# A two-layer decoder trunk on one core: the evictions and the split weights beside the RWKV-7 recurrence, kept in the order of emission

## The chip, the cores and the metric

The kernel runs on 1 core of a Trainium2 chip. The metric is device time in microseconds (us) of one execution; lower is better. TensorE is PE in the profile, VectorE is DVE, ScalarE is ACT, GpSimd is POOL and SyncE, whose queue issues most of the transfers, is SP.

## The reference, cut to what matters

The trunk has two layers of width 1024 over 1024 positions, batch 1, in float32. Layer 0 mixes tokens with a gated MLP, layer 1 with RWKV-7 time mixing; each layer then has a squared-ReLU MLP (1024 to 4096 to 1024). The change is about layer 1's mixer:

```python
def rwkv7_mixer(h, mu, w_in, w0, w1, w2, a0, a1, a2, g1, g2, k_k, k_a, r_k, ln_g, ln_b, w_out):
    xx = token_shift(h) - h
    xr, xw, xk, xv, xa, xg = [h + xx * mu[i] for i in range(6)]
    r, k, v = xr @ w_in[:, 0], xk @ w_in[:, 1], xv @ w_in[:, 2]
    w_log = -jax.nn.softplus(-(w0 + jnp.tanh(xw @ w1) @ w2)) - 0.5
    a = jax.nn.sigmoid(a0 + (xa @ a1) @ a2)
    g = jax.nn.sigmoid(xg @ g1) @ g2
    ...
    # for each head of 64, state S (64 x 64), over all positions:
    #   S = S * w_t + (S a_t) b_t^T + v_t k_t^T ;  y_t = S r_t
    y = wkv7_scan(rh, decay, kh, vh, -kk, kk * ah)
    ...
    return (y * g) @ w_out
```

## The kernel before

**Numbers in two parts.** PE multiplies float32 values in a rounded form. So that the large products keep their precision, each weight tile and each activation tile is split into a rounded part (`hi`) and the rest (`lo`), and three matmuls (hi by hi, hi by lo, lo by hi) stand for one. A *piece* is a 128x512 weight tile. To split one on chip, `split_piece` casts it (`wh`, on ACT or every third time on DVE, L401) and subtracts (`wl`, on DVE or POOL in turn, L407).

**Layer 1's mixer works on four quarters q of 256 positions.** `jobs` (L810) lists the products of a quarter: `big` (r, k, v, four jobs `m` each), `hidden` (the first factor of w, a or g) and `outs` (the second factor). Each gathers its inputs from `mixes` (token-shifted blends, DVE and POOL, split by `split_pair` into `xi`), multiplies into a PSUM bank named `acc` (two buffers), and `out2` evicts the bank into an `ev` tile (three buffers, L931 and L989) and stores it in DRAM. `outp` multiplies the recurrence's gated output, which `gated` loads from DRAM (`ev<-yd`, L995), with the last weight.

**The weights of the mixer are used once in each quarter.** `presplit` therefore splits all 80 pieces of quarter 0 ahead, beside the end of layer 0, and stores both parts in DRAM (`split`, from the tiles `ada_acc` and `araw`, L336, L355, L358). From quarter 1 on `load_split` (L326) brings both parts back: two transfers of 256 KB for one piece, and no work of another engine.

**The recurrence runs beside these products.** `wkv` cuts it into 16 units (a quarter q and four heads, m). A unit is a set of generators: `unit_a` prepares the factors, `unit_s` inverts 16x16 triangular blocks on DVE (15 steps `pr`, `tb`, between a round trip through DRAM: `ltd<-la`, `lb<-ltd`, then `tpd<-tb`, `t<-tpd`, `pf<-tpd`), `unit_b` joins the blocks, `unit_c` runs four chunks of 64 positions in three steps each, and `unit_d` normalises and stores. In `unit_c` a step is: matmuls into the bank `c`, its eviction (`xs`, then `uv`, then the new state `S`), and the next step's matmuls read that.

**What sets the order.** `interleave` (L1211) holds a heap of the generators by due time, counted in units; each `yield` names the next due time, and a step is 1/13 of a unit (`SLOT`). Time goes forward by the nominal cost of the product work that it emits in between, `RATES` us of it to a unit (28.0 for the first ten units, 41.5 after). PE's instructions keep this order of emission (`Pinned`). Those of all other engines are ordered by a scheduler, which may move them past each other where no data forbid it. After the products come the second MLP's first blocks for the first half of positions (`half0`), then the rest of that MLP alone.

Of the kernel before, what the change touches and what calls it, by code (L numbers as in the profile page):

```python
# [16 lines left out]
P = 128  # L17
# [91 lines left out]
class Trunk:  # L109
# [219 lines left out]
    def presplit(self, todo, pool):  # L329
# [9 lines left out]
        todo = list(zip(todo, self.split_ahead))  # L339
# [28 lines left out]
    def make_split(self, dp):  # L368
# [9 lines left out]
        self.split_ahead = kept  # L378
        at = lambda kind, q: [j for j in self.jobs() if j[:2] == (kind, q)]
# [6 lines left out]
        self.order_split = [p for kind, _, name, m in self.parts()[1] for p in kept[place[kind, name, m]]]  # L386
# [423 lines left out]
    def jobs(self):  # L810


        for q in range(self.NQ):
            for name, low in ("vw", "ra", "kg"):
                for m in range(4):
                    yield "big", q, name, m
                    if m in (1, 2):
                        yield ("hidden", "outs")[m - 1], q, low, 0
        for q in range(2):
            for m in range(4):  # L820
                yield "outp", q, "", m
# [7 lines left out]
    def pieces(self, jobs):  # L829
# [3 lines left out]
        for kind, q, name, m in jobs:  # L833
# [12 lines left out]
            else:  # L846
                for h in range(2):
                    cs = slice(h * 512, h * 512 + 512)
                    if name == "g":
                        yield [a["b_g2"][:P, cs]], 0, None  # L850
                        yield [a["b_g2"][P:, cs]] * 3, 0, slice(64, 96)
                    else:
                        yield [a[f"b_{name}2"][:, cs]] * 2, 0, None
# [108 lines left out]
    def outs(self, q, name, _):  # L962
        nc = self.nc
        bias = {"w": self.w0h, "a": self.a0h, "g": None}[name]
        for m in range(4):
            if m % 2 == 0:
                wh, wl = self.piece()
                if name == "g":
                    gst, _ = self.piece()
# [215 lines left out]
    RATES = [28.0] * 10 + [41.5]  # L1185
# [25 lines left out]
    def interleave(self, gens, bg):  # L1211
# [4 lines left out]
        now = 0.  # L1216
        while live:
            due, n, t, g = live[0]
            if now < due:
                c = next(bg, None)  # L1220
                now = float("inf") if c is None else now + max(c, .01) / self.RATES[min(int(now), len(self.RATES) - 1)]
                continue
            try:
                heapq.heapreplace(live, [t + next(g), n, t, g])
            except StopIteration:
                heapq.heappop(live)

# [54 lines left out]
    def unit_a(self, d):  # L1282
# [39 lines left out]
        yield 0.2  # L1322
# [7 lines left out]
        yield 0.21  # L1330
        S.activation(rn, rn, AF.Exp, scale=-0.5)
        yield 0.25
# [3 lines left out]
        yield 0.28  # L1336
# [35 lines left out]
    def unit_e(self, d, z):  # L1372
# [10 lines left out]
        for c in range(4):  # L1383
            cc = (z * 4 + c) * 2
            PE.transpose(pt[:, c * P:(c + 1) * P], bk[:, cc:cc + 2].rearrange("p a t -> p (a t)"), self.ident)
        S.copy(tm[:, qc], pt.rearrange("p (c t) -> p c t", t=P))
# [17 lines left out]
    def unit_s(self, d):  # L1404
# [10 lines left out]
        yield 0.68  # L1415
        for i in range(1, NB):
# [6 lines left out]
            yield 0.68 + .017 * i  # L1423
        V.tensor_copy(tb[:, 1], tb[:, 0].rearrange("p s k -> p k s"))
        yield 0.96
# [3 lines left out]
        yield 1.0  # L1429
# [14 lines left out]
    def unit_b(self, d):  # L1444
# [15 lines left out]
        yield at(3) + .005  # L1460
# [3 lines left out]
        pw = self.ps("t")  # L1464
        pr, pq = cut(pw, 16), cut(pw[:, P:], 16)
# [5 lines left out]
        yield at(4) + .005  # L1471
# [12 lines left out]
        yield at(5) + .005  # L1484
# [10 lines left out]
        yield at(6) + .005  # L1495
        for s in self.HS:
            a, b = s.start, s.start + 32
            (S.copy if b > 64 else V.tensor_copy)(pf[a:b, :, 32:], pr[a:b])

    def unit_c(self, d):  # L1500
# [11 lines left out]
        for c in range(4):  # L1512
# [40 lines left out]
            yield step(3 * c + 3) if c < 3 else step(11) + .01  # L1553
# [240 lines left out]
```

## Time and profile before

| | |
|---|---|
| time, median of 3 runs | 2800.86 us (2793.97 to 2807.12) |
| the profiled execution's own time | 2805.26 us |
| its span, from the first to the last instruction | 2803.5 us |
| mean granted TensorE clock | 0.969 |
| PE busy | 2613.3 us, 93% |
| DVE, ACT, POOL busy | 1638.3, 1146.9, 544.7 us |
| moved by DMA | 483.67 MB, mean 173 GB/s |

The profile is of one execution. PE is busy when any matmul is in flight. The granted clock is the share of full speed at which TensorE was let run: it has two levels, 0.5 (1.2 GHz) and 1.0 (2.4 GHz), and a mean over a stretch tells how much of it was at the lower one. An engine's instructions run in its queue's order, so one that waits holds up all that stand behind it. The program's stages by time: layer 0's first mixer to 476 us, its MLP from there to about 1040 us with the splitting ahead beside it until 755 us, the mixer's quarter 0 until 1226 us, the recurrence with quarters 1 to 3 until about 1715 us, with `outp` and `half0` until 2340 us, and the rest of the second MLP to the end.

### The profile page before, as it was taken

What the parts mean: (1) busy time and instruction counts of PE and PEld (TensorE: products, weight loads), DVE (VectorE), ACT (ScalarE), POOL (GpSimd) and SP (SyncE); (2) the same over time, 40 slices, a digit from 0 to 9 for tenths busy, and PEclk for the clock granted to TensorE, in tenths of its full rate; (3) what the DMA queues carried; (4) which work ended last, traced back from release to release, by engine and by line L of the source; (5) the groups of instructions that cost most, each with busy time, mean ns of one, the idle gap of its engine ahead of it and who ended that gap; (6) DMA issues with size and microseconds to landing.
All of it is one profiled execution on the core that took longest, in us unless ns stands there. A gap on an engine that the chain in (4) does not pass through costs nothing.

```text
span 2803.5 us, 49454 instructions
## 1 busy us (share of the span) xinstructions
PE 2613.3 (93%) x19020; PEld 2152.6 (77%) x19020; DVE 1638.3 (58%) x3066; ACT 1146.9 (41%) x2074; POOL 544.7 (19%) x574
## 2 busy tenths in 40 slices
PE   6999999999999999787898997879999999999998
PEld 4788888877888788787787886777777778788887
DVE  7856775444333458866666663566667545744445
ACT  4523442333311344553454543464444334533333
POOL 1000000433300013431322231123334220100001
PEclk9999999999999999998999999899999999999999
DMA  7644545888711354788888889753333324333332
GB/s 279 211 142 128 167 155 163 274 278 255 237 49 49 91 165 138 241 291 261 260 284 265 270 289 274 211 149 110 104 104 100 91 86 151 103 109 94 95 94 83
DMA packets 369708, 483.67 MB, mean 173 GB/s; under 512 B 144320, under 2 KB 153536, under 8 KB 368704
## 3 DMA queue, kind: packets, MB, share of 16 engines
q1 hardware_dynamic: 354496, 454.18, 52.3%
q10 hardware_dynamic: 14976, 26.34, 2.5%
q8 instruction: 149, 2.44, 0.4%
q14 instruction: 87, 0.71, 0.1%
HBM read 390.07 MB, written 90.32 MB: 171 GB/s over the span
## 4 chain that ended last, share of the span: by engine, by line
PE 67%; DVE 12%; DMA 11%; ACT 4%; issue 4%; SPq 1%; POOL 1%; ACTq 0%; DVEq 0%; POOLq 0%
PE acc L448 24%; PE acc L646 15%; PE acc L103 15%; PE c L103 2%; PE acc L503 2%; DMA split<-ada_acc 2%; PE t L103 2%; DMA split<-araw 2%; DVE pr L1420 2%; DVE hm L874 2%; PE acc L894 1%; DVE wl L407 1%; DMA araw<-in_ada_w 1%; DVE xi L440 1%; DMA lb<-ltd 1%
## 5 line engine op out<-in xcount | busy, mean ns | idle before, releaser
L448 PE MATMUL acc<-h,wh 128*128 128x512 f32 x2112 | 667.4, 397 | 0.0
L401 ACT CAST wh<-raw 128x512 fp32r<-128x512 f32 x517 | 318.6, 619 | 732.6 <-PE acc L448 299.0
L646 PE MATMUL acc<-s,wh 128*128 128x512 f32 (+1 forms) x1664 | 510.4, 389 | 12.1 <-DVE s L439 9.1
L407 DVE TENSOR_TENSOR wl<-raw,wh 128x512 fp32r<-128x512 f32 x475 | 363.1, 767 | 264.4 <-ACT wh L401 259.3
L448 PEld LDWEIGHTS acc<-h,wh 128*128 128x128 f32 x2112 | 394.9, 188 | 94.5 <-issue 1.2
L448 PE MATMUL acc<-h,wl 128*128 128x512 f32 x1056 | 418.0, 396 | 0.0
L646 PEld LDWEIGHTS acc<-s,wh 128*128 128x128 f32 x1664 | 308.9, 189 | 86.5 <-DVE s L439 14.8
L646 PE MATMUL acc<-s,wl 128*128 128x512 f32 (+1 forms) x832 | 323.1, 389 | 0.5 <-DVE wl L407 0.5
L452 DVE SCALAR_TENSOR_TENSOR x<-acc,mod,x 128x512 f32<-128x512 f32 (+1 forms) x224 | 163.1, 730 | 231.0 <-PE acc L646 206.4
L448 PEld LDWEIGHTS acc<-h,wl 128*128 128x128 f32 x1056 | 198.4, 188 | 48.0 <-issue 0.5
L103 PE MATMUL acc<-s,wh 128*128 128x512 f32 (+1 forms) x616 | 188.0, 390 | 35.0 <-ACT s L437 18.3
L407 POOL TENSOR_TENSOR wl<-raw,wh 128x512 fp32r<-128x512 f32 (+1 forms) x107 | 145.6, 1363 | 318.2 <-ACT wh L401 156.2
L103 PE MATMUL acc<-xi,wh 128*128 128x256 f32 (+1 forms) x896 | 179.5, 300 | 10.0 <-ACT hm L954 5.2
L646 PEld LDWEIGHTS acc<-s,wl 128*128 128x128 f32 x832 | 157.5, 189 | 35.3 <-DVE wl L407 1.2
L358 POOL TENSOR_TENSOR araw<-araw,ada_acc 128x512 fp32r<-128x512 f32 (+1 forms) x78 | 101.2, 1300 | 389.4 <-ACT ada_acc L355 354.1
L103 PEld LDWEIGHTS acc<-s,wh 128*128 128x128 f32 x616 | 111.0, 196 | 62.8 <-ACT s L437 18.8
L103 PEld LDWEIGHTS acc<-xi,wh 128*128 128x128 f32 (+1 forms) x896 | 144.3, 198 | 17.7 <-ACT hm L954 5.4
L103 PE MATMUL acc<-h,wh 128*128 128x512 f32 (+1 forms) x512 | 150.7, 381 | 3.2 <-ACT ev L1057 3.2
L103 PE MATMUL acc<-xi,wl 128*128 128x256 f32 (+1 forms) x448 | 129.8, 290 | 1.6 <-issue 0.8
L355 ACT CAST ada_acc<-araw 128x512 fp32r<-128x512 f32 (+1 forms) x80 | 49.4, 618 | 168.4 <-DMA split<-ada_acc 124.3
L103 PE MATMUL acc<-s,wl 128*128 128x512 f32 (+1 forms) x308 | 114.9, 373 | 0.0
L157 DVE SCALAR_TENSOR_TENSOR ada_acc<-araw,cond,ada_acc 128x512 f32<-128x512 f32 x140 | 104.4, 746 | 13.0 <-DMA araw<-in_ada_w 11.1
(269 smaller groups left out, 4415.8 us busy)
## 6 DMA issues: line engine op xcount, KB each, us to landing
raw<-in_mlp_w SPq DMA_DIRECT2D x432, 256.0 KB, 2.7
araw<-in_ada_w SPq DMA_DIRECT2D x192, 256.0 KB, 3.5
raw<-split SPq DMA_DIRECT2D x142, 256.0 KB, 4.9
wh<-split SPq DMA_DIRECT2D x141, 256.0 KB, 4.6
wl<-split SPq DMA_DIRECT2D x141, 256.0 KB, 4.7
split<-ada_acc SPq DMA_DIRECT2D x76, 256.0 KB, 3.8
split<-araw SPq DMA_DIRECT2D x76, 256.0 KB, 4.1
araw<-in_w_in SPq DMA_DIRECT2D x48, 256.0 KB, 3.8
```

Source lines behind the costliest of these rows:

```text
L103: self.tc.keep_in_program_order(self.pe.matmul(*a, **k))
L157: nc.vector.scalar_tensor_tensor(acc, raw, self.cond[:, k:k + 1], acc, ALU.mult, ALU.add)
L355: nc.scalar.copy(hi[:rows, :m].bitcast(F32R), raw[:rows, :m])
L358: nc.gpsimd.tensor_tensor(to[lo, :m].bitcast(F32R), raw[lo, :m], hi[lo, :m], ALU.subtract)
L401: (nc.vector.tensor_copy if self.nhi % 3 == 0 and self.shared else nc.scalar.copy)(wh[:rows], raw[:rows])
L407: eng.tensor_tensor(wl[:rows], raw[:rows], rd(wh[:rows]), ALU.subtract)
L448: nc.tensor.matmul(ps, w[s](k), x[m][:, k], start=n == 0, stop=n == 3 * KC - 1)
L452: self.nc.vector.scalar_tensor_tensor(x[:, e], ps, gate[:, e:e + 1], x[:, e], ALU.mult, ALU.add)
L503: self.nc.tensor.matmul(ps, h[s][:, k, ts], self.wv[k][m], start=k + i == 0, stop=k + i == KC + 1)
L646: nc.tensor.matmul(ps, w[:, k], s[hf, k][:, i, ts], start=n == 0, stop=n == 3 * FB - 1)
L874: nc.vector.scalar_tensor_tensor(t[:, z], self.hx[:, e + z], self.mu[:, i, e + z:e + z + 1], self.h[:, e + z, 1:], ALU.mult, ALU.add)
L1420: V.tensor_tensor(pr[:, :i, :i], lb[:, 0:i, i].unsqueeze(1).to_broadcast([64, i, i]), tb[:, 0, 0:i, 0:i].rearrange("p s k -> p k s"), ALU. ...
```

## The change

It has five parts, all for the stretch in which the recurrence runs.

1. `pin` in `interleave`: each DVE, ACT and POOL instruction emitted there must follow, on its engine, the one emitted before it. The scheduler no longer reorders these three engines there. SP's transfers are not pinned.
2. Evictions are emitted later: extra `yield`s (+.012 of a unit, that is one more piece of product work) between a bank's matmuls and its eviction in `unit_c`, `unit_b`, `unit_e`; the triangular inverse starts at .745 of a unit and not .68, and hands over at 1.06 and not 1.0; some due times of `unit_a` move by .01 to .02.
3. One engine for each bank: the copies `uv`, `w1` and `pf`, of which DVE did one half of the partitions and ACT the other, are all ACT's; `pr` and `pq` get a bank each.
4. Fewer pieces are split ahead: of the pieces without repeats (`rep` 1) every second one (33 of the 80: 24 of `big`, 1 of `hidden`, 8 of `outp`) is left out of `presplit`, loaded raw each time, and split on chip by `split_piece`.
5. `outs` is cut into two jobs of two evictions each, after m = 2 and after m = 3 (before: one job of four evictions after m = 2). `RATES` becomes 27.3 and 42.5.

```diff
-        todo = list(zip(todo, self.split_ahead))
+        todo = [p for n, p in enumerate(zip(todo, self.split_ahead)) if n not in self.again]
...
+        self.again = {n for n, p in enumerate(self.whole) if p[1] == 1 and n % 2}
...
-        self.order_split = [p for kind, _, name, m in self.parts()[1] for p in kept[place[kind, name, m]]]
+        self.order_split = [self.whole[n] if n in self.again else kept[n]
+                            for kind, _, name, m in self.parts()[1]
+                            for n in range(place[kind, name, m].start, place[kind, name, m].stop)]
...
-                    if m in (1, 2):
-                        yield ("hidden", "outs")[m - 1], q, low, 0
+                    if m:
+                        yield "outs" if m > 1 else "hidden", q, low, max(m - 2, 0)
...
-    RATES = [28.0] * 10 + [41.5]
+    RATES = [27.3] * 10 + [42.5]
...
+        def pin():
+
+            nonlocal seen
+            assert nc.cur_bb is bb
+            ins = bb.bb.instructions
+            for i in ins[seen:]:
+                if i.engine in (E.DVE, E.Activation, E.Pool):
+                    if i.engine in last:
+                        self.tc.add_manual_dep(i, last[i.engine], mybir.DependencyInfo(
+                            mybir.DependencyClass.NoSync, mybir.DependencyReason.DATA), reason="order")
+                    last[i.engine] = i.name
+            seen = len(ins)
...
-        yield 0.68
+        yield 0.745
...
-        yield 1.0
+        yield 1.06
...
-        pw = self.ps("t")
-        pr, pq = cut(pw, 16), cut(pw[:, P:], 16)
+        pr, pq = cut(self.ps("t"), 16), cut(self.ps("r"), 16)
...
-            (S.copy if b > 64 else V.tensor_copy)(w[b:b + 32], pw[b:b + 32])
+            S.copy(w[b:b + 32], pw[b:b + 32])
...
+            yield step(3 * c) + .012
             xs = self.ups[1].tile([P, 2, CS], F32, name="xs", bufs=2)
...
+            yield step(3 * c + 1) + .012
             for z in Z:
-                (S.copy if z else V.tensor_copy)(uv[ss[z], z * 4 + c], pu[ss[z]])
+                S.copy(uv[ss[z], z * 4 + c], pu[ss[z]])
...
+            yield step(3 * c + 2) + .012
             for z in Z:
                 V.scalar_tensor_tensor(ns[z], pq[:, z * CS:z * CS + CS], gc[z], sg[z], ALU.mult, ALU.add)
```

The first place is ACT's queue in the second half of a unit (`xs`, `uv`: the recurrence's evictions; `xi`: a product's input; in brackets what each waits for, after the engine's or queue's name). Before:

```order
L437 CAST xi<-hm 128x512 [waits PE_49] x2
L1526 COPY xs<-c 128x128 [waits PE_49]
L931 COPY ev<-acc 128x512 [waits DMAHW2_49,PE_49]
L922 DMA sdk_8599<-ev 128x512 [waits DMAHW5_49,Activation_49]
L437 CAST xi<-hm 128x512 [waits DVE_49] x2
L1540 COPY uv_13518<-c 64x128 [waits DVE_49]
```

With the change:

```order
L1550 COPY xs<-c 128x128 [waits PE_49]
L441 CAST xi<-hm 128x512 [waits DVE_49]
L405 CAST wh<-raw 128x512 [waits DMAHW2_49,DMAHW0_49,PE_49]
L441 CAST xi<-hm 128x512 [waits DVE_49]
L1565 COPY uv_12440<-c 64x128 [waits PE_49]
L1565 COPY uv_12440<-c 64x128
```

Both halves of `uv` stand together and wait for PE instead of DVE; a weight's cast has come between, and the casts of `xi`, two at a time before, stand one by one.

The second place is POOL's queue over about half a unit (`sg`: the decayed state of a chunk; `k`, `bk`, `ar`, `ysq`: the recurrence's factors and its output). Before:

```order
L1584 TENSOR_TENSOR ysq<-ysq,gt 128x512
L1530 TENSOR_SCALAR sg<-S,g_11806 128x64 x2
L1315 TENSOR_SCALAR k_13568<-wa,kah,ka_8534 128x256 x2
L1316 TENSOR_TENSOR k_13568<-k_13568,k 128x512
L1329 TENSOR_TENSOR bk<-k_13568,gi 128x2x128
L1329 TENSOR_TENSOR bk<-k_13568,gi 128x2x2x64
L1530 TENSOR_SCALAR sg<-S,g_11806 128x64 x4
```

With the change:

```order
L1610 TENSOR_TENSOR ysq<-ysq,gt 128x512
L411 TENSOR_TENSOR wl<-raw,wh 128x512
L1554 TENSOR_SCALAR sg<-S,g_12436 128x64 x2
L411 TENSOR_TENSOR wl<-raw,wh 128x512
L1318 MEMSET g_14157 128x8
L1554 TENSOR_SCALAR sg<-S,g_12436 128x64 x2
L1338 TENSOR_SCALAR k_14234<-wa,kah,ka_8303 128x256 x2
L1339 TENSOR_TENSOR k_14234<-k_14234,k 128x512
L411 TENSOR_TENSOR wl<-raw,wh 128x512
L1352 TENSOR_TENSOR bk<-k_14234,gi 128x2x128
L1352 TENSOR_TENSOR bk<-k_14234,gi 128x2x2x64
```

Three subtractions for weights have come between the recurrence's own steps.

The third place is SP's queue where `outp` begins (`hm<-xd`: four loads of the first half of x, 512 KB each, into the space that the mixes leave; `ev<-yd`: the gated output that the first product of `outp` reads). Before:

```order
L1428 DMA tpd_257<-tb 64x16x16 x2
L326 DMA wl<-split_1_232 128x512
L1133 DMA hm<-xd 128x1024
L1433 DMA t<-tpd_257 64x8x64 x2
L1433 DMA pf_17741<-tpd_257 64x8x64 x2
L1133 DMA hm<-xd 128x1024 x3
L995 DMA ev<-yd_8607 128x512 x3
```

With the change:

```order
L1135 DMA hm<-xd 128x1024
L326 DMA raw<-split_1_223 128x512
L1591 DMA gt<-sdg_8363 128x512
L326 DMA wh<-split_0_224 96x512
L305 DMA raw<-in_b_w_out 128x512
L1452 DMA tpd_257<-tb 64x16x16 x2
L326 DMA wh<-split_0_225 128x512
L326 DMA wl<-split_1_226 128x512
L1457 DMA t<-tpd_257 64x8x64 x2
L1457 DMA pf_17634<-tpd_257 64x8x64 x2
L326 DMA raw<-split_0_229 128x512
```

The last of the four loads of x stands here ahead of the round trip of `tpd` (the other three stand 18 to 26 places further ahead); `ev<-yd` follows two transfers behind these rows.

## Rows read from the trace of the kernel before

**Rows 1.** The page: the span, and PE's busy time.

```profile
span 2803.5 us, 49454 instructions
PE 2613.3 (93%) x19020; PEld 2152.6 (77%) x19020; DVE 1638.3 (58%) x3066; ACT 1146.9 (41%) x2074; POOL 544.7 (19%) x574
```

**Rows 2.** Windows by stage: stretch, busy us of PE, PEld, DVE, ACT, POOL, clock, DMA.

```profile
476.00:720.00 244.00, 234.18 (x993) 187.14 (x993) 107.02 (x128) 84.71 (x147) 89.52 (x69) 0.99 0.82 263
1040.00:1226.00 186.00, 160.06 (x984) 141.92 (x982) 146.45 (x219) 87.12 (x155) 79.81 (x80) 0.92 0.63 193
1226.00:1715.00 489.00, 431.19 (x5767) 388.99 (x5766) 298.07 (x735) 240.07 (x476) 127.47 (x152) 0.94 0.87 278
1715.00:1950.00 235.00, 183.37 (x2157) 158.02 (x2156) 128.15 (x309) 107.53 (x217) 58.34 (x70) 0.88 0.60 177
1950.00:2340.00 390.00, 382.82 (x3700) 292.64 (x3699) 237.78 (x523) 160.51 (x305) 131.81 (x139) 1.00 0.37 105
```

**Rows 3.** Waits of PE, 1226 to 1715 us: us in total, times, longest.

```profile
PE acc L103 <- ACT ev L989: 10.8, 8, 3.0
PE t L103 <- DMA t<-tpd: 9.8, 2, 9.4
PE c L103 <- DVE S L1551: 9.0, 7, 2.7
PE c L103 <- ACT uv L1540: 5.9, 3, 3.0
PE acc L103 <- ACT ev L931: 5.3, 5, 2.8
```

**Rows 4.** Waits of PE, 1715 to 1950 us.

```profile
PE acc L103 <- ACT s L437: 20.2, 3, 17.2
PE acc L103 <- DVE hm L452: 10.4, 9, 2.9
```

**Rows 5.** Waits of ACT and of DVE, 1226 to 1715 us.

```profile
ACT uv L1540 <- DVE uv L1540: 55.1, 27, 6.5
...
DVE tb L1418 <- DMA lb<-ltd: 24.5, 5, 6.2
DVE xi L440 <- ACT xi L437: 22.4, 12, 8.5
```

**Rows 6.** Groups by line, 1226 to 1715 us: busy us, mean ns, idle before.

```profile
L1540 DVE COPY uv<-c 64x128 f32<-64x128 f32 x28 | 8.0, 285 | 29.7 <-PE c L103 29.5
L1540 ACT COPY uv<-c 64x128 f32<-64x128 f32 x28 | 7.3, 259 | 55.1 <-DVE uv L1540 55.1
```

**Rows 7.** Timeline of SP at the start of `outp`: start, us.

```profile
1740.95 2.63 SPq L1133 DMA_DIRECT2D hm<-xd  x3
1743.68 1.52 SPq L995 DMA_DIRECT2D ev<-yd  x3
```

**Rows 8.** Timeline of PE at the same place, and at 686 us.

```profile
1751.08 1.31 PE L103 MATMUL acc<-s,wh 128*128 128x256 f32 x2 [17.18 <-ACT s L437]
...
686.20 0.49 PE L646 MATMUL acc<-s,wh 128*128 128x512 f32 x1 [3.92 <-DVE s L439]
```

**Rows 9.** The casts of the splitting ahead, by source line.

```profile
L355 ACT CAST ada_acc<-araw x80: 513/620/627, 488.9 to 755.0; 128x512 fp32r<-128x512 f32 x76, 128x384 fp32r<-128x384 f32 x2, 96x512 fp32r<-96x512 f32 x2
```

**Rows 10.** Groups, 1090 to 1226 us: every piece is split on chip there.

```profile
L894 PE MATMUL acc<-xi,wl 128*128 128x256 f32 (+1 forms) x184 | 57.0, 310 | 17.9 <-DVE wl L407 10.1 <-POOL wl L407 7.7
L407 POOL TENSOR_TENSOR wl<-raw,wh 128x512 fp32r<-128x512 f32 (+1 forms) x29 | 39.6, 1371 | 64.9 <-ACT wh L401 41.9 <-DVE wh L401 18.5 <-PE acc L980 2.8
L401 ACT CAST wh<-raw 128x512 fp32r<-128x512 f32 (+2 forms) x39 | 23.6, 613 | 23.3 <-DMA raw<-in_w_in 8.1 <-PE acc L894 5.0 <-DMA raw<-in_mlp_w 3.8
```

**Rows 11.** Timeline of ACT: the first and last of one pair of table loads.

```profile
1755.78 1.28 ACT L1324 ACT_TABLE_LOAD   x1
...
1759.08 0.63 ACT L1331 ACTIVATE rn<-rn 128x512 f32<-128x512 f32 x1
```

**Rows 12.** One DVE instruction of each unit, 1226 to 1715 us: first and last start.

```profile
L1309 DVE TENSOR_TENSOR_SCAN wa<-rmask,wa x9: 1204/1220/1225, 1248.4 to 1714.8; 128x512 f32<-128x512 f32 x9
```

**Rows 13.** Transfers of weights, 1226 to 1715 us: KB each, us to landing.

```profile
raw<-split SPq DMA_DIRECT2D x113, 256.0 KB, 4.9
wh<-split SPq DMA_DIRECT2D x113, 256.0 KB, 4.7
```

More of the change, by code (lines that the diff above doesn't have):

```diff
@@ L846, in pieces @@
             else:
[L847 to L853, printed above, removed]
+                cs = slice(m * 512, m * 512 + 512)
+                if name == "g":
+                    yield [a["b_g2"][:P, cs]], 0, None
+                    yield [a["b_g2"][P:, cs]] * 3, 0, slice(64, 96)
+                else:
+                    yield [a[f"b_{name}2"][:, cs]] * 2, 0, None
     def load_h(self, q):
@@ L960, in hidden, with outs @@
                 nc.vector.tensor_tensor(gh[32:64, 2], s[32:64], rd(gh[32:64, 2]), ALU.subtract)
-    def outs(self, q, name, _):
+    def outs(self, q, name, part):
         nc = self.nc
         bias = {"w": self.w0h, "a": self.a0h, "g": None}[name]
[L965 to L969, printed above, removed]
+        wh, wl = self.piece()
+        if name == "g":
+            gst, _ = self.piece()
+        for m in range(2 * part, 2 * part + 2):
             ps, half = self.acc2()
@@ L1216, in interleave @@
         now = 0.
+        nc = self.nc
+        E = mybir.EngineType
+        last, bb = {}, nc.cur_bb
+        seen = len(bb.bb.instructions)
+        def pin():
[9 more added lines that the diff above has]
+            seen = len(ins)
         while live:
@@ L1221, in interleave @@
                 now = float("inf") if c is None else now + max(c, .01) / self.RATES[min(int(now), len(self.RATES) - 1)]
+                pin()
                 continue
@@ L1226, in interleave @@
                 heapq.heappop(live)
+            pin()
+        pin()
     def after(self, ins):
@@ L1321, in unit_a @@
         S.activation(g[:, :, 1:], c8(ew), AF.Exp, scale=-E)
-        yield 0.2
+        yield 0.18
         with self.after(self.last_ln):
@@ L1329, in unit_a @@
             G.tensor_tensor(bv[:, js, at], c2(k2)[:, js], c2(gi)[:, js], ALU.mult)
-        yield 0.21
+        yield 0.19
         S.activation(rn, rn, AF.Exp, scale=-0.5)
-        yield 0.25
+        yield 0.27
         V.scalar_tensor_tensor(kk, rn, 1e12 * 2.0 ** 8, kk, ALU.min, ALU.mult)
@@ L1335, in unit_a @@
         V.scalar_tensor_tensor(b2, kk, 2.0 ** -9, gi, ALU.mult, ALU.mult)
-        yield 0.28
+        yield 0.295
         for js, at in ((slice(0, 2), outer), (slice(2, 4), inner)):
@@ L1385, in unit_e @@
             PE.transpose(pt[:, c * P:(c + 1) * P], bk[:, cc:cc + 2].rearrange("p a t -> p (a t)"), self.ident)
+        yield t0 + .015
         S.copy(tm[:, qc], pt.rearrange("p (c t) -> p c t", t=P))
@@ L1422, in unit_s @@
             V.tensor_reduce(tb[:, 0, i, 0:i], pr[:, :i, :i], AX.X, ALU.add)
-            yield 0.68 + .017 * i
+            yield 0.745 + .017 * i
         V.tensor_copy(tb[:, 1], tb[:, 0].rearrange("p s k -> p k s"))
-        yield 0.96
+        yield 1.02
         td = self.tpd[d["n"] % 2]
@@ L1459, in unit_b @@
                           start=True, stop=True)
-        yield at(3) + .005
+        yield at(3) + .015
         w = self.ups[0].tile([P, 8, 16], F32, name="w0")
@@ L1470, in unit_b @@
                 PE.matmul(pq[a:a + 32, c], pf[a:a + 32, c, :32], w[a:a + 32, c], start=True, stop=True)
-        yield at(4) + .005
+        yield at(4) + .015
         for a, b in blocks[::2]:
@@ L1483, in unit_b @@
                 PE.matmul(pw[b:b + 32, c], lt(slice(a, b), c)[:, 32:], t[a:b, c, :32], start=True, stop=True)
-        yield at(5) + .005
+        yield at(5) + .015
         w = self.ups[0].tile([P, 8, 32], F32, name="w1")
@@ L1494, in unit_b @@
                 PE.matmul(pr[a:b, c], w[b:b + 32, c], pf[b:b + 32, c, 32:], start=True, stop=True)
-        yield at(6) + .005
+        yield at(6) + .015
         for s in self.HS:
             a, b = s.start, s.start + 32
-            (S.copy if b > 64 else V.tensor_copy)(pf[a:b, :, 32:], pr[a:b])
+            S.copy(pf[a:b, :, 32:], pr[a:b])
     def unit_c(self, d):
@@ L1552, in unit_c @@
             st = ns
-            yield step(3 * c + 3) if c < 3 else step(11) + .01
+            yield step(3 * c + 3) if c < 3 else step(11) + .025
         y = d["y"] = self.late("y")
```

## The prediction

> **What bounds the kernel now.** I read the page first: PE is busy for 2613.3 of 2803.5 us [rows 1], so no more than about 190 us of waiting can be won, and the count of matmuls does not change. Then the windows by stage, which tell where that waiting is [rows 2]. Look at PE's busy time and at the clock. Up to 1040 us there is little (476 to 720 us: 244.0 - 234.2 = 9.8 us idle). From 1226 to 1715 us, the recurrence beside quarters 1 to 3, PE idles 489.0 - 431.2 = 57.8 us, and the granted clock is 0.94: of 431 busy us some 6% is work done at 1.2 GHz that full speed would have saved, 26 us. From 1715 to 1950 us it is 51.6 us idle at 0.88, so 22 us more. From 1950 to 2340 us PE idles 7.2 us at full clock: PE itself is the bound. The clock falls behind idle time in these rows, so I charge each idle us there with 83.8 / 57.8 = 1.45 us. No other engine is the bound: between 1226 and 1715 us DVE is busy 61%, ACT 49%, POOL 26%. DMA, at 0.87, is the fullest, but PE hardly waits for weights.
>
> Then PE's waits in these two stretches. In the first they are many and short [rows 3]: evictions of `outs` (10.8 us), one late `t` (9.4 of 9.8 us), the recurrence's `S` and `uv` (14.9 us together), evictions of `big` (5.3 us); these are 40.8 of 57.8 us. In the second, one wait of 17.2 us stands out, where `outp` begins, and nine short ones on the residual [rows 4].
>
> **The change, part by part**, with minus for time saved.
>
> *Fewer pieces split ahead.* 80 casts take from 488.9 to 755.0 us, 3.33 us a piece [rows 9]; 47 pieces end near 645 us. The 33 casts, 33 subtractions, 66 stores and 33 loads that go lie beside PE's work and cost nothing, since ACT is busy only 35% there [rows 2]. What they do cost is the stall at 686 us, 3.92 us [rows 8], where a cast that waits for its store holds up ACT. It falls behind the new end: 3.92 x 1.45 = **-6**. Ends: 0 (the stall comes back elsewhere) and -14 (all 9.8 us).
>
> *One engine for a bank.* The two halves of `uv` take 0.285 us on DVE and then 0.259 us on ACT, in series: ACT stood still 55.1 us, 27 times, for DVE's half, 2.0 us each [rows 5, 6]. On ACT alone a pair is 0.52 us, with no handing over. PE's waits on `uv` and `S` are 14.9 us [rows 3]; I take half, 7.5 x 1.45 = **-11**; ends 0 and -22. ACT gets one more copy of 0.26 us for each pair, 7 us in the stretch, hidden by its 51% of idle time; if that cover went, the copy would be on the recurrence's chain. The Trainium skill (PSUM — Partial Sum Buffer, "PSUM bank collisions raise a hardware error") speaks against this part: two engines may be in one bank at once if they are in different quadrants of 32 partitions, and the halves are, so a pair on two engines would need only the longer copy. The trace does not show that use: ACT's half waits for DVE's. By that rule the pair would go from 0.285 to 0.52 us, 6.5 us over 28 pairs, and this term would be about zero.
>
> *`outs` in halves.* Four evictions in a row meet three `ev` tiles and two banks; two and two do not. I take two thirds of the 10.8 us: 7 x 1.45 = **-10**; ends 0 and -16.
>
> *The order.* The trace of before cannot show it. In the best case all other short waits go (57.8 - 10.8 - 9.8 - 14.9 = 22.3 us, -32). In the other direction the engines are coupled: each `xi` subtraction on DVE now stands right behind its cast on ACT, as the first place of the order shows. DVE waits so 12 times now, 22.4 us, 1.9 us each [rows 5]; 64 such casts fall into the stretch, and 64 x 1.9 = 120 us of waiting would fit into DVE's 191 us of idle time, but if a tenth reaches PE it costs +17. I take **-14**, nearer to the first end, since three engines then serve PE's needs in PE's own order. Later evictions belong here: an eviction emitted one product piece later finds its matmuls done and does not hold its queue.
>
> *The triangular inverse later.* DVE waited 24.5 us, 5 times, for `lb` [rows 5], 4.9 us each, and in a fixed order all its work stands behind that. A unit lasts (1714.8 - 1248.4) / 8 = 58.3 us [rows 12], so .065 of it is 3.8 us: most of the wait is covered. At the other end, `t` has from 1.06 to 1.23 of a unit, 9.9 us, where it had 13.4. I take **0**; ends -14 (the late `t` comes in time, with fewer transfers ahead of it) and +14.
>
> *Weights split on chip.* Per quarter 25 of the mixer's 64 pieces in the three quarters, 75 in all, become one transfer instead of two (so about 19 MB fewer, on a queue that is hidden anyway [rows 13]), one cast and one subtraction. Where every piece is split, PE idled 17.9 us ahead of 184 lo matmuls, four to a piece, so 46 pieces and 0.39 us a piece [rows 10]. 75 pieces at that price are 29 us, +42 with the clock; the low end is 0. With 39% of the pieces split I take 0.4 of it: **+17**. POOL gets about half of the subtractions, 1.37 us each, between the recurrence's steps (second place of the order), ACT two thirds of the casts, 0.61 us: 30 us more, to 55% with `uv`.
>
> *The start of `outp`.* All engines stand for 17.18 us [rows 8]. `ev<-yd` is issued behind three loads of x, 2.63 us, and PE starts 1751.08 - 1743.68 = 7.4 us after its issue [rows 7, 8], against 4.7 to 4.9 us that a transfer takes to land in the stretch before [rows 13]. With x loaded further ahead I take 2.6 + 2.5 us off, -7; eight of 16 pieces of `outp` are split, twice: 16 x 0.39 x 0.5 = 3 us, +4; and of the other 24 us idle (51.6 - 17.2 - 10.4) the order takes a third, 8 x 1.4 = -11. Together **-14**; ends +5 and -45. The round trip of `tpd` still stands ahead of `ev<-yd`, so the wait will not go altogether.
>
> *1950 to 2340 us.* PE is full; the fixed order can only add there: **+4**, ends 0 and +20. The new `RATES` shift 0.7 us of product work a unit from the first ten units to the later ones; PE's work is the same, so 0.
>
> **The sum**: -6 - 11 - 10 - 14 + 17 - 14 + 4 = -34 us against the profiled execution's 2805.3 us, 2771 us. The median of the runs lies 4.4 us lower, so it is 2767 us there; I say **2768 us**.
>
> **The rivals.**
>
> *The order clears the waits.* The many short waits have one cause, that a queue holds something PE needs later ahead of what it needs now, and two thirds of the loss of both stretches go: 0.67 x (83.8 + 73.6) = 105 us, less 21 us for the splitting, plus 6: -90, 2715 us. For it: nearly every wait of rows 3 is on an eviction of under 0.6 us. Against: the tables and DRAM round trips stay. 18%.
>
> *Nothing comes of it.* The scheduler's order was much like the emission order already, the new subtractions take what the evictions give, and other engines' waits change without reaching PE: within 14 us, about 2800 us. For it: of the engines' waits, only a few reach PE (55 us on ACT's `uv`, 5.9 us on PE). 15%.
>
> *Slower: the pairs of table loads block the chain.* ACT is held 1759.71 - 1755.78 = 3.93 us by two table loads with their activations [rows 11]; `unit_a` and `unit_d` each have one such pair a unit. A step of the recurrence is 58.3 / 13 = 4.48 us. If in the fixed order an eviction stands right behind a pair with more than 0.55 us of other work ahead of it (a weight's cast alone is 0.61 us [rows 10]), it comes late, and DVE, behind its `xi`, with it. One eviction a unit late by the 2.0 us of today's `uv` waits [rows 5], times 1.45, over 16 units, is +47 us; less 23 us for the parts that do not hang on it (-6, -10, -7): 2829 us. For it: ACT gets more work and may not slip it past the loads any more. Against: the pairs stood in the queue before, with half of the chain's copies on DVE. 17%.
>
> **How the numbers follow.** My forecast, 2745 to 2787 us, has 50%. A difference of 0.5%, 14 us, is about what a measurement of this kernel can tell. The range goes from the first rival's time to shortly under the slower one's: 2712 to 2818 us; outside lie most of the slower case and a little below. Faster: 50 + 18, less 2 for a forecast that ends short, 66%; same 17%; slower 17%.
>
> **What would show it.** Right: no wait of ACT's `uv` on DVE; PE's idle time between 1226 and 1715 us at 40 to 50 us with a clock of 0.95 or more; the splitting ahead over near 645 us; 10 us instead of 17 at the start of `outp`; DMA under 0.80 in the stretch. Wrong: new PE waits on `wl` above 12 us, DVE waits for ACT's `xi` above 60 us that reach PE, or waits on `xs` and `uv` right behind table loads; and, for the first rival, idle time under 25 us.

## The result and the profile after

The changed kernel is slower: 2845.58 us, median of 4 runs (2840.74 to 2850.98), beside 2801.9 us for the kernel before on the same chip (4 runs). The ratio is 1.0153, with a 95% interval of 1.0128 to 1.0178. The prediction was 2768 us, range 2712 to 2818.

The profiled execution took 2840.74 us. Its page (the answer to [rows 1]) shows the same work over a longer span:

```profile
span 2838.7 us, 49377 instructions
PE 2639.0 (93%) x19020; PEld 2177.2 (77%) x19020; DVE 1668.7 (59%) x3046; ACT 1186.9 (42%) x2199; POOL 575.3 (20%) x586
```

The matmul count is the same, but PE's busy time is 25.7 us longer, at a mean granted clock of 0.956 against 0.969: more of the matmuls ran at the lower clock. Of the 35.2 us by which the span grew this is the larger part; PE's idle time grew by 9.5 us, from 190.2 to 199.7. The windows of [rows 2], with the same columns:

```profile
476.00:720.00 244.00, 243.27 (x1050) 195.65 (x1049) 103.54 (x136) 74.66 (x128) 61.62 (x47) 1.00 0.61 197
1040.00:1226.00 186.00, 157.32 (x989) 143.37 (x987) 137.80 (x203) 87.59 (x154) 65.98 (x50) 0.87 0.62 195
1226.00:1715.00 489.00, 410.71 (x5148) 365.62 (x5149) 315.71 (x708) 247.34 (x514) 161.62 (x176) 0.88 0.70 214
1715.00:1950.00 235.00, 186.60 (x2252) 166.59 (x2248) 129.39 (x304) 120.83 (x250) 71.95 (x74) 0.85 0.58 175
1950.00:2340.00 390.00, 383.85 (x3968) 295.30 (x3967) 242.88 (x504) 178.34 (x362) 151.97 (x154) 1.00 0.37 103
```

Where fewer pieces are split ahead PE's idle time fell from 9.8 to 0.7 us. Beside the recurrence it rose from 57.8 to 78.3 us and the granted clock fell from 0.94 to 0.88. The windows are fixed in time and not in work: from 1226 to 1715 us the changed kernel did 5148 matmuls, the kernel before 5767. In the next stretch idle time fell a little, 51.6 to 48.4 us, at a lower clock, 0.85 against 0.88. One instruction of each unit (the answer to [rows 12]) gives the period: (1768.8 - 1272.4) / 8 = 62.1 us against 58.3.

```profile
L1332 DVE TENSOR_TENSOR_SCAN wa<-rmask,wa x9: 1224/1225/2175, 1272.4 to 1768.8; 128x512 f32<-128x512 f32 x9
```

PE's waits from 1226 to 1715 us answer to [rows 3]; the last two rows of the fence are those from 1715 to 1950 us [rows 4]:

```profile
PE r L103 <- ACT ysq L1583: 15.8, 2, 11.5
PE c L103 <- ACT uv L1565: 9.1, 4, 4.0
PE acc L103 <- ACT wh L405: 7.8, 6, 3.1
PE acc L103 <- ACT ev L991: 6.9, 7, 2.2
PE acc L103 <- POOL wl L411: 5.7, 7, 1.3
PE t L103 <- DMA t<-tpd: 4.4, 4, 1.6
...
PE acc L103 <- DVE hm L456: 19.9, 9, 5.8
PE acc L103 <- ACT s L441: 12.1, 4, 5.3
```

The long `t` and the 17.2 us at the start of `outp` are gone, and `outs`' evictions cost less. New are `ysq` (a unit's squared output, an eviction of the recurrence) and the weights' casts; the residual took 19.9 us instead of 10.4. Behind them stand waits of ACT and DVE from 1226 to 1715 us:

```profile
ACT xi L441 <- DVE hm L877: 109.1, 45, 7.1
...
DVE xi L444 <- ACT xi L441: 65.8, 60, 5.5
DVE la L1387 <- PE m L103: 20.5, 6, 6.8
DVE tb L1442 <- DMA lb<-ltd: 18.0, 7, 7.8
```

The first and the third of these before:

```profile
ACT xi L437 <- DVE hm L874: 42.6, 24, 7.6
...
DVE la L1364 <- PE m L103: 4.0, 4, 2.8
```

The second was 22.4 us [rows 5]; all three have grown. The last, the wait for `lb`, was 24.5 us [rows 5] and fell.

The largest new wait of PE can be followed through the queues. The timeline of SP, POOL, DVE, ACT and PE where the activations of the next quarter are loaded (start, us; in brackets the idle time before, and its releaser):

```profile
1352.65 0.56 SPq L862 DMA_DIRECT2D hm<-hd  x1
1361.16 3.22 POOL L874 TENSOR_TENSOR hm<-hm 128x512 f32<-128x512 f32 x3 [2.08 <-DMA hm<-hd]
1362.24 2.42 DVE L877 SCALAR_TENSOR_TENSOR hm<-hm,mu 128x256 f32<-128x256 f32 x2 [6.59 <-POOL hm L874]
1364.75 0.62 ACT L441 CAST xi<-hm 128x512 fp32r<-128x512 f32 x1 [7.11 <-DVE hm L877]
1367.79 0.62 ACT L441 CAST xi<-hm 128x512 fp32r<-128x512 f32 x1 [2.43 <-DVE hm L877]
1370.55 0.59 ACT L1581 COPY y<-y 128x512 f32<-128x512 f32 x1
1371.03 0.60 ACT L1583 ACTIVATE ysq<-y 128x512 f32<-128x512 f32 x1
1371.69 2.08 PE L103 MATMUL r<-ysq,bones 128*128 128x512 f32 x2 [11.47 <-ACT ysq L1583]
```

The load of h is a transfer of the products. POOL waits for it, DVE waits 6.59 us for POOL, ACT 7.11 us for DVE, and the recurrence's `y` and `ysq`, which stand behind `xi` on ACT in the order of emission, come late: PE stands 11.47 us. The Trainium skill (PSUM — Partial Sum Buffer, "Engine vs sequencer instructions") says that the queues of ACT, DVE and POOL are strictly first in, first out; this trace agrees.

### The profile page after: what moved, and what is told of

It reads as the page before. It is cut to its first block, busy times and chain, and to the rows that moved or that the text cites. A ratio compares the mean times of both kernels' runs of the same rounds, so it can differ in the third digit from the quotient of the medians.

```text
span 2838.7 us, 49377 instructions
## 1 busy us (share of the span) xinstructions
PE 2639.0 (93%) x19020; PEld 2177.2 (77%) x19020; DVE 1668.7 (59%) x3046; ACT 1186.9 (42%) x2199; POOL 575.3 (20%) x586
## 4 chain that ended last, share of the span: by engine, by line
PE 71%; DVE 13%; ACT 6%; DMA 5%; issue 3%; POOL 1%; SPq 1%; ACTq 0%; DVEq 0%; POOLq 0%
PE acc L452 27%; PE acc L650 18%; PE acc L103 14%; PE c L103 2%; PE acc L507 2%; DVE hm L877 2%; DVE pr L1444 2%; DVE wl L411 2%; PE acc L897 2%; PE t L103 1%; PE g L103 1%; DVE tb L1446 1%; ACT xi L441 1%; DVE xi L444 1%; DVE wh L405 1%
## 5 line engine op out<-in xcount | busy, mean ns | idle before, releaser
L405 ACT CAST wh<-raw 128x512 fp32r<-128x512 f32 x578 | 355.0, 618 | 715.9 <-PE acc L452 317.0
L411 DVE TENSOR_TENSOR wl<-raw,wh 128x512 fp32r<-128x512 f32 x521 | 391.8, 754 | 269.0 <-ACT wh L405 256.8
L411 POOL TENSOR_TENSOR wl<-raw,wh 128x512 fp32r<-128x512 f32 x152 | 216.6, 1427 | 731.7 <-ACT wh L405 417.4
L650 PEld LDWEIGHTS acc<-s,wh 128*128 128x128 f32 x1664 | 306.6, 188 | 75.1 <-DVE s L443 5.3
L103 PE MATMUL acc<-xi,wh 128*128 128x256 f32 (+1 forms) x1080 | 225.1, 308 | 22.1 <-ACT wh L405 9.2
L103 PE MATMUL acc<-s,wh 128*128 128x512 f32 (+1 forms) x664 | 198.7, 384 | 24.1 <-ACT s L441 12.1
L103 PEld LDWEIGHTS acc<-xi,wh 128*128 128x128 f32 (+1 forms) x1080 | 179.9, 206 | 33.1 <-ACT wh L405 10.7
L103 PE MATMUL acc<-xi,wl 128*128 128x256 f32 (+1 forms) x540 | 161.9, 300 | 11.1 <-POOL wl L411 5.7
L103 PEld LDWEIGHTS acc<-s,wh 128*128 128x128 f32 x664 | 121.4, 200 | 49.8 <-ACT s L441 13.0
L441 ACT CAST xi<-hm 128x512 fp32r<-128x512 f32 x96 | 59.1, 617 | 157.6 <-DVE hm L877 141.7
L358 POOL TENSOR_TENSOR araw<-araw,ada_acc 128x512 fp32r<-128x512 f32 (+1 forms) x45 | 59.0, 1316 | 320.8 <-ACT ada_acc L355 306.6
L103 PEld LDWEIGHTS acc<-xi,wl 128*128 128x128 f32 (+1 forms) x540 | 111.1, 206 | 14.9 <-POOL wl L411 7.3
```

The costliest lines, as they stand in the source:

```text
L103: self.tc.keep_in_program_order(self.pe.matmul(*a, **k))
L358: nc.gpsimd.tensor_tensor(to[lo, :m].bitcast(F32R), raw[lo, :m], hi[lo, :m], ALU.subtract)
L405: (nc.vector.tensor_copy if self.nhi % 3 == 0 and self.shared else nc.scalar.copy)(wh[:rows], raw[:rows])
L411: eng.tensor_tensor(wl[:rows], raw[:rows], rd(wh[:rows]), ALU.subtract)
L441: nc.scalar.copy(hi, src)
L650: nc.tensor.matmul(ps, w[:, k], s[hf, k][:, i, ts], start=n == 0, stop=n == 3 * FB - 1)
```

## The experiments

Each kernel was timed beside the kernel before on one chip. Ratios are to that, in brackets the 95% interval. First, two parts of the change were taken out of it and put alone into the kernel before.

**All pieces split ahead (the change without part 4).**

```diff
-        self.again = {n for n, p in enumerate(self.whole) if p[1] == 1 and n % 2}
+        self.again = set()
```

> The change with all 80 pieces split ahead again, as before; the fixed order, the later evictions, ACT alone for each bank, outs in halves and RATES stay. Theory A (the raw pieces' splitting on chip, beside the recurrence, is what costs): the stretch from the first pinned product to outp loses the waits on wh and wl (24 us of PE's idle time there, and as much again by the clock), so about 2800 to 2815 us, although the splitting ahead takes back its 10 to 13 us. Theory B (the fixed order of ACT, DVE and POOL is what costs): 2845 to 2860 us. Theory C (the moved due times and the single engine cost): as B.

Measured: 2822.42 us, 1.0062 [1.0040, 1.0084].

**No fixed order (the change without part 1).**

```diff
-                if i.engine in (E.DVE, E.Activation, E.Pool):
+                if i.engine in ():
```

> The change without the fixed order: the scheduler orders DVE, ACT and POOL as before, everything else of the change stays. Theory A: 2835 to 2850 us, no different from the change. Theory B: 2785 to 2810 us, with the waits on ysq, uv and rr behind other engines' work gone. Theory C: about 2840 us.

Measured: 2805.34 us, 1.0005 [0.9987, 1.0023].

**The kernel before with part 4 alone** (the first two pieces of the change's diff).

> The kernel before with one part of the change, the 33 pieces left raw and split on chip. Theory A: 2825 to 2845 us, slower by the splitting's 40 to 50 us less 10 to 13 us for the splitting ahead. Theory B or C: 2785 to 2800 us, a small gain at the splitting ahead and small costs beside the recurrence.

Measured: 2830.43 us, 1.0095 [1.0064, 1.0126].

**The kernel before with part 1 alone** (`pin`).

> The kernel before with one part of the change, the fixed order (evictions as early as before, two engines for a bank, all pieces split ahead). Theory A: 2795 to 2815 us. Theory B: 2835 us or more, since evictions that are emitted right behind their matmuls now hold their queues as well. Theory C: about 2800 us.

Measured: 2919.34 us, 1.0414 [1.0392, 1.0437]. The first run lies between what A and B expected; the second and the fourth fit B, the third A. Both the pieces split on chip and the fixed order cost, with or without the rest. The fixed order costs 4.1% without the other parts and 1.5% with them, so some of the others make it bearable.

Next, neither of the two, and each engine in order by itself.

**Neither.** Both edits of the first two runs together.

> The change without its fixed order and without its raw pieces: later evictions, one engine for a bank, the outs in halves and the new rates are left. If the costs of raw pieces (0.9%) and of the fixed order (1.5%) simply add up, those four parts gain what is left: 1.0153 - 0.009 - 0.015 = 0.991, about 2780 us, faster than both kernels. If both costs have one cause (any more work in the recurrence's queues, so that taking either away clears most of it), it stays at 0.998 to 1.002, about 2805 us.

Measured: 2794.16 us, 0.9964 [0.9947, 0.9981]. This lies between the two expectations. The remaining parts gain less than the sum of ratios promised: without a fixed order the raw pieces cost the change 0.4%, not 0.9%. In the kernel before, where no order is fixed either, they cost 0.95%, so their price does not hang on the order alone.

```diff
-                if i.engine in (E.DVE, E.Activation, E.Pool):
+                if i.engine in (E.Activation,):
```

(and with `E.DVE`, `E.Pool` in its place).

> The change with ACT alone in order of emission; DVE and POOL are left to the scheduler. With no engine in order the ratio was 1.0005, with all three 1.0153. Theory 'ACT': the engine that evicts for the recurrence is held by casts of xi and of weights; then this run alone has most of the cost, 1.010 to 1.015. Theory 'POOL': the wait for the loads of h is the start of it, and ACT alone costs under 0.4%: 1.000 to 1.004. Theory 'coupling': the cost comes from three queues that wait for each other in turn, no one of them alone has more than a third of it, under 1.0055.

> The change with DVE alone in order of emission. Theory 'ACT': 1.000 to 1.003. Theory 'POOL': 1.000 to 1.004. Theory 'coupling': under 1.0055. A fourth possibility, that DVE's triangular inverse behind a DRAM round trip holds all of DVE's work, would put most of the cost here: 1.010 or more.

> The change with POOL alone in order of emission. Theory 'POOL' (the blends of h wait on POOL for the loads of h, and the recurrence's work behind them stands): most of the cost, 1.008 to 1.015. Theory 'ACT': 1.000 to 1.003. Theory 'coupling': under 1.0055.

Measured: ACT alone 2817.68 us, 1.0050 [1.0028, 1.0072]; DVE alone 2857.21 us, 1.0197 [1.0165, 1.0229]; POOL alone 2792.44 us, 0.9957 [0.9935, 0.9979]. "ACT", "POOL" and "coupling" all fall: DVE's order is the costly one, POOL's even gains. The stall on `ysq` that was followed above comes with ACT's order (with DVE alone in order it is 0.9 us). With ACT alone in order, from 1226 to 1715 us:

```profile
PE r L103 <- ACT ysq L1583: 12.1, 3, 8.6
```

PE's waits with DVE alone in order, in the same window:

```profile
PE acc L103 <- DVE wl L411: 17.9, 8, 5.8
PE acc L103 <- DVE wh L405: 14.9, 3, 9.0
PE c L103 <- DVE S L1577: 11.7, 9, 4.0
PE g L103 <- DVE rr L1388: 10.5, 4, 4.6
```

The same four without any order:

```profile
PE c L103 <- DVE S L1577: 19.5, 10, 5.4
...
PE acc L103 <- DVE wh L405: 5.9, 1, 5.9
...
PE g L103 <- DVE rr L1388: 2.3, 2, 1.3
PE acc L103 <- DVE wl L411: 1.8, 3, 1.1
```

With DVE in order PE waits 32.8 us for the weights' halves, which the products read, and 22.2 us for the recurrence's `S` and `rr`. Without it these are 7.7 and 21.8 us, so most of what is new is the wait for the products' work. PE's waits on `rr` and `ar` ahead of the bank `m`, the recurrence's again, went from 1.2 to 11.4 us.

What on DVE does it? DVE's subtractions for `xi` wait for ACT 60 times, so they were the first suspect, and the inverse behind its DRAM round trip the second.

**`xi`'s subtractions, or the inverse, left to the scheduler; `xi`'s subtractions emitted one step later.** All three are the change with a few edits (`free` holds names of instructions that `pin` skips):

```diff
-                if i.engine in (E.DVE, E.Activation, E.Pool):
+                if i.engine in (E.DVE, E.Activation, E.Pool) and i.name not in self.free:
```

For the third, `split_pair` emits only the cast, and the subtraction follows at the next call of `ahead`, `mt` or `mix_set`:

```diff
-        self.split(hl[:, 0], hl[:, 1], t)
+        self.nc.scalar.copy(hl[:, 0], t)
+        self.rest = hl, t
...
+    def flush_xi(self):
+        if self.rest:
+            hl, t = self.rest
+            self.rest = None
+            self.nc.vector.tensor_tensor(hl[:, 1], t, rd(hl[:, 0]), ALU.subtract)
```

> The change, all three engines in order of emission, but DVE's subtraction for xi (64 of them in the stretch, each right behind its own cast on ACT) is left to the scheduler. Theory D: DVE pays, since it stands 1.1 us at each of 67 casts of xi (73.1 us in the change, 22.1 us over 11 times without the fixed order), and the recurrence's S, w and tb stand behind it. Then most of the fixed order's cost goes: from 1.0153 to 1.003 or less. Theory I: it is the inverse (tb, pr) behind its DRAM round trip; then 1.012 or more. Theory O: order on DVE as such, many small waits; then 1.008 to 1.012.

> The change, but the triangular inverse on DVE (pr, tb: some 30 instructions a unit, which begin behind lb from DRAM) is left to the scheduler, all else in order of emission. Theory I: most of the fixed order's cost goes, 1.003 or less. Theory D: 1.012 or more, at the best 1.01 (lb held DVE for 18.2 us, 8 times). Theory O: 1.008 to 1.012.

> The change in full, all three engines in order, but each subtraction for xi is emitted one step of the products later (some 12 matmuls behind its cast), the change's own idea for evictions applied to xi. Theory D: DVE finds the cast done, and the time falls as in the run that leaves xi to the scheduler, 1.003 or less. Theory I and O: no fall, 1.012 or more; or only a part, 1.008 to 1.012.

Measured: 2831.78 us, 1.0111 [1.0086, 1.0136]; 2841.01 us, 1.0136 [1.0118, 1.0155]; 2842.75 us, 1.0136 [1.0115, 1.0157]. Neither suspect carries the cost. Leaving `xi` free takes 0.4% of the 1.5% away, as theory O expected; the other two take 0.2% each, within the uncertainty. In the third, DVE's waits from 1226 to 1715 us were:

```profile
DVE la L1400 <- PE m L103: 29.7, 8, 7.3
DVE xi L895 <- ACT xi L885: 28.6, 28, 3.6
DVE wl L411 <- ACT wh L405: 24.3, 17, 4.3
```

The waits on `xi` fell from 65.8 to 28.6 us, those on `la` rose from 20.5 to 29.7 and those on `wl` from 12.3 to 24.3. So 21.2 of the 37.2 us came back under other names.

**Two chains on each engine.** `pin` keeps the order among the products' instructions and among the recurrence's, and lets the scheduler move the one past the other:

```diff
-        def pin():
+        def pin(kind):
...
-                    if i.engine in last:
+                    if (i.engine, kind) in last:
...
-                pin()
+                pin(0)
                 continue
...
-            pin()
-        pin()
+            pin(1)
+        pin(1)
```

> The change, all three engines in order, but in two chains on each: the products' instructions (weights split, blends, xi, evictions to ev) keep their order among themselves, the recurrence's keep theirs, and the scheduler may move the one past the other. Theory X (the cost comes from the products' work and the recurrence's standing behind each other's waits): most of the fixed order's 1.5% goes, 1.004 or less. Theory W (the order inside one of the two is at fault, such as la and tb behind each other in the recurrence, or wl behind xi in the products): 1.010 or more. Between them both have a part.

> The two chains with all 80 pieces split ahead. By theory X 0.992 to 0.998, at the level of the runs without a fixed order and without raw pieces (0.9964) or better; by theory W 1.002 to 1.008, near the full order without raw pieces (1.0062).

Measured: 2801.64 us, 0.9995 [0.9979, 1.0011]; without raw pieces 2773.61 us, 0.9899 [0.9863, 0.9934]. Theory X holds: without any order the ratio was 1.0005, so the whole 1.5% goes when the products' and the recurrence's instructions need no longer stand behind each other. On which of the three engines this matters was not tried. The group of the unit's instruction, and DVE's longest wait from 1226 to 1715 us, with two chains:

```profile
L1332 DVE TENSOR_TENSOR_SCAN wa<-rmask,wa x9: 1205/1224/1226, 1267.1 to 1728.5; 128x512 f32<-128x512 f32 x9
...
DVE xi L444 <- ACT xi L441: 41.5, 37, 4.0
```

A unit takes 461.4 / 8 = 57.7 us, though DVE still waits 41.5 us for `xi`. And the timeline at the load of h:

```profile
1345.36 0.59 ACT L1581 COPY y<-y 128x512 f32<-128x512 f32 x1
1345.84 0.61 ACT L1583 ACTIVATE ysq<-y 128x512 f32<-128x512 f32 x1
1350.87 0.62 ACT L441 CAST xi<-hm 128x512 fp32r<-128x512 f32 x1 [4.42 <-DVE hm L877]
...
1357.02 1.22 PE L103 MATMUL acc<-xi,raw 128*128 128x256 f32 x4 [6.98 <-ACT hm L957]
```

ACT still waits for DVE's blend, but `y` and `ysq` are through before it. PE's stall at this place is 6.98 us, on a product, instead of 11.47 us.

**POOL alone in order, no raw pieces.**

> The change with POOL alone in order of emission and all 80 pieces split ahead: the best of each part by the runs so far. If the gains add (POOL in order 0.9957 against 1.0005 with none; no raw pieces 0.9964 against 1.0005): 0.9957 x 0.9964 / 1.0005 = 0.992, about 2782 us. If POOL's order only helped with the raw pieces' subtractions, which are gone here: 0.9964, about 2795 us.

Measured: 2787.2 us, 0.9947 [0.9928, 0.9966]; the interval holds the second expectation, 0.9964, and just misses the first, 0.992.

**What gains.** The rates alone, the three parts on evictions alone (the change without parts 1 and 4 and with the old rates), the halves alone, and the rates with two chains but without those three parts.

```diff
-    RATES = [28.0] * 10 + [41.5]
+    RATES = [27.3] * 10 + [42.5]
```

> The kernel before with the new RATES alone. The prediction said 0. If the shift of work from the first ten units to the later ones is what the four remaining parts gain (0.9964 in the run with neither pin nor raw pieces), it gives 0.996 to 0.998; if the gain is that of the later evictions, the single engine and the halves, it gives 0.999 to 1.001.

> The kernel before with the later evictions, the single engine for a bank and the outs in halves; no fixed order, no raw pieces, the old RATES. The prediction took -21 us for these (-11, -10 and 0): 0.9925. By the runs, with the rates the same parts stand at 0.9964 and the rates alone at 0.9923, so without them 1.004: the three parts gain nothing where the scheduler is free.

> The kernel before with the outs in halves alone. The prediction took -10 us, 0.9965; if the waits of PE on these evictions only move to other places, 0.999 to 1.002.

> The kernel before with the new RATES and the order kept in two chains on each engine (products and recurrence apart); no later evictions, no single engine, no halves, no raw pieces. If the rates (0.9923) and the two chains (0.9899 with them against 0.9964 without, 0.9935) both carry over: 0.986, about 2765 us. If a fixed order inside the recurrence needs the later evictions (the full order without them cost 4.1%, with them 1.5%): 1.00 or more.

Measured: rates 2781.36 us, 0.9923 [0.9892, 0.9953]; evictions 2811.01 us, 1.0038 [1.0022, 1.0055]; halves 2817.54 us, 1.0064 [1.0040, 1.0088]; rates and two chains 2812.04 us, 1.0029 [1.0008, 1.0051]. The rates gain more than was expected, the three parts came out as expected, and the halves cost more than either expectation. The last one fits its second expectation: beside the rates alone the two chains cost 1.1% there. Beside the run with two chains and the eviction parts (0.9899) it shows what these are good for: without a fixed order they cost 0.4%, with the two chains they are worth 1.3%.

The windows with the rates alone:

```profile
1226.00:1715.00 489.00, 438.45 (x5891) 396.86 (x5891) 313.83 (x774) 247.09 (x493) 127.56 (x157) 0.94 0.90 283
1715.00:1950.00 235.00, 196.02 (x2248) 166.54 (x2250) 138.94 (x335) 109.04 (x221) 68.89 (x75) 0.90 0.60 180
1950.00:2340.00 390.00, 385.47 (x3634) 296.54 (x3633) 232.27 (x490) 164.63 (x310) 127.21 (x131) 1.00 0.38 109
```

Idle time of PE is 50.6 + 39.0 + 4.5 = 94.1 us, against 57.8 + 51.6 + 7.2 = 116.6 us [rows 2]: 22.5 us less, about what was measured; 12.6 us of it lie from 1715 to 1950 us. PE's waits with the halves alone, 1226 to 1715 us:

```profile
PE t L103 <- DMA t<-tpd: 15.2, 6, 8.1
PE acc L103 <- ACT hm L953: 13.2, 2, 7.7
PE acc L103 <- ACT ev L930: 12.6, 8, 2.8
...
PE acc L103 <- ACT ev L987: 5.6, 4, 3.0
```

The evictions of `outs` (10.8 us before) are 5.6 us, as meant, but those of `big` went from 5.3 to 12.6 us, and `t` from 9.8 to 15.2 us [rows 3]. A part of the loss lies earlier, in quarter 0:

```profile
1040.00:1226.00 186.00, 156.12 (x927) 138.25 (x926) 141.88 (x209) 83.05 (x148) 78.77 (x79) 0.88 0.56 178
```

PE did 927 matmuls there instead of 984; it was idle for 29.9 us instead of 25.9, at a clock of 0.88 instead of 0.92 [rows 2].

## Why the prediction was wrong

The runs build the change up step by step. Ratios times 2803 us give its cost beside the prediction's terms (each step is a difference of two ratios, with 7 to 10 us of uncertainty at 95%; the -14 of the start of `outp` stands whole in the row of the order, though 4 and -7 of it are for pieces and for the loads of x):

| step | ratio after it | measured, us | predicted, us |
|---|---|---|---|
| rates | 0.9923 | -21.6 | 0 |
| later evictions, one engine, halves | 0.9964 | +11.5 | 0 - 11 - 10 = -21 |
| raw pieces, fewer split ahead | 1.0005 | +11.5 | +17 - 6 = +11 |
| the fixed order | 1.0153 | +41.5 | -14 - 14 + 4 = -24 |
| sum | | +42.9 | -34 |

**The order: the step that failed.** The term for the order was -14 us, -21 with its -11 at the start of `outp` and its +4 after 1950 us; the order cost 41.5 us. The prediction took it nearer to its good end, "since three engines then serve PE's needs in PE's own order". PE's order is one of two programs interleaved, and each of them has waits that the other need not share: transfers of h, a DRAM round trip, casts on another engine. In one queue each waits for both. The bad end was priced from DVE's waits for `xi` alone, at a tenth of 120 us. These waits did come (65.8 us, 60 times, near the 64 that were counted), yet they were not the price: with `xi` left free 1.0111 remains, and with two chains 41.5 us of the waits stay and the cost is gone. What counts is what stands behind a wait, and that is not in the row of the wait. The stall on `ysq` is the one case that was followed through the queues; on DVE, whose order costs most, the runs show the price and not each step of it.

**The clock charge was too small as well.** An idle us was charged with 1.45. From 1226 to 1715 us the change has 78.3 us idle and (1 - 0.88) x 410.7 = 49.3 us of clock, 1.63 to one. Against the kernel before, 20.5 us more idle time came with about 23 us more of clock.

**The raw pieces: a right sum of two terms that were both too small.** +11 us was predicted and measured in the change without its order. The end of the splitting ahead was right (near 645 us), but it gave more than the -6 of the one stall. From 476 to 720 us 2.8 us of idle time are left without the order and 0.7 us with it, where 9.8 were; the first is an estimate of 7.0 x 1.45 = 10 us. The splitting on chip then took some 21 us, not 17, and that the sum fits is in part luck. The price also changes with the rest of the kernel: 0.95% in the kernel before, 1.0153 - 1.0062 = 0.9% (25 us) under the fixed order, 0.4% in the change without it. Why was not followed. ACT's busy share in the stretch was added up wrongly, without effect on the sum: (240.1 + 30 + 7) / 489 is 57%, not 55%. The row that answers to [rows 9]:

```profile
L355 ACT CAST ada_acc<-araw x47: 513/621/626, 489.5 to 640.8; 128x512 fp32r<-128x512 f32 x43, 128x384 fp32r<-128x384 f32 x2, 96x512 fp32r<-96x512 f32 x2
```

**`outs` in halves had the wrong sign:** -10 predicted, 0.0064 x 2803 = +18 us measured. The step "two and two do not" meet full buffers was right for these evictions (10.8 to 5.6 us), but left out what is late next: 10.8 + 5.3 us of waits on `ev` became 5.6 + 12.6. That is 2 us more and `t` 5 us more, not 18; the prediction also gave quarter 0 no price, where idle time and clock came to 29.9 + 0.12 x 156.1 = 48.6 us against 25.9 + 0.08 x 160.1 = 38.7.

**One engine for a bank.** ACT's waits for DVE's half of `uv` (55.1 us) are gone, as predicted. They were not the price of handing over, as the prediction read them: DVE's half itself stood 29.5 us for PE [rows 6]. Together with the later evictions the part is worth 1.0038 - 1.0064, -7 us, within the uncertainty of two runs; -11 was taken. Against it the prediction weighed the rule of the Trainium skill that two engines may use different quadrants of one bank at the same time (PSUM — Partial Sum Buffer, "PSUM bank collisions raise a hardware error"), and by it came to about 0; the runs do not separate the two.

**The rates were wrong.** "PE's work is the same, so 0": the work is, but its idle time is not, 22.5 us less in the three windows. Why a shift of 0.7 us a unit does this was not followed further.

**The start of `outp`.** The three waits on `s` from 1715 to 1950 us, 20.2 us with the one of 17.2 [rows 4], became four of 12.1 us, of which none is over 5.3; 10 us were expected for the long one alone. The run without a fixed order has 11.9 us, so this gain is not the order's:

```profile
PE acc L103 <- ACT s L441: 11.9, 3, 6.0
PE acc L103 <- DVE hm L456: 8.2, 9, 2.0
```

The residual, 10.4 us before and 8.2 us here, rose to 19.9 us under the fixed order, and to 17.7 us with two chains: this loss the chains do not take back.

**The slower rival** had the size (2829 us, still 17 below) and not the mechanism. It lives by ACT's order, and ACT alone in order costs 1.0050 - 1.0005 = 0.45%, 13 us, where the rival had 47; DVE alone in order, with ACT's loads and casts free, costs 1.9%. In the two chains the pairs of table loads keep their fixed place among the recurrence's evictions and the cost is gone, though a weight's cast, which the rival also needs ahead of the eviction, may step aside there.

**The signs.** Of those for being right, `uv`, the end near 645 us and DMA under 0.80 (0.70) came, idle time (78.3 us) and clock (0.88) did not. Of those for being wrong DVE's waits for `xi` came (65.8 us, over 60); PE's waits on `wl` stayed at 9.2 us, under 12.

## What to carry to other kernels

When two streams of work share in-order queues and their order is to be fixed, fix each stream's by itself; fixing their interleaving makes each wait for both, and a wait's price is what stands behind it. Even then a fixed order is no gain by itself: it cost 1.1% with the early evictions and gained 0.65% with the later ones (0.9899 against 0.9964, all pieces split ahead). The parts on evictions cost 0.4% where the scheduler is free and are worth 1.3% with two fixed chains, so judge such parts in the setting in which they will run. The two fastest versions are the rates alone (0.9923) and two chains with the later evictions and all pieces split ahead (0.9899); their intervals overlap.

## What the runs showed that was not expected

The price of idle time through the clock is no constant of this kernel: idle and clock together came to 1.63 us for an idle us in the changed kernel, and to (50.6 + 0.06 x 438.5) / 50.6 = 1.52 with the rates alone. And one engine's order is enough for all of the cost: over the run with no order (1.0005) ACT's alone costs 0.45%, DVE's 1.9% and POOL's -0.5%, 1.9% in sum, all three together 1.5%. DVE's alone is no cheaper than all three; whether the three add up or help each other a little, these runs cannot tell.
